# Left operands of the block products loaded into the tile of their low part, and a fourth raw tile for the right operands

## The chip, the core and the metric

The kernel runs on one core of a Trainium2 chip. Five engines work side by side on the core: TensorE (matrix products), VectorE (called DVE in the profile), ScalarE (ACT), GpSimd (POOL) and SyncE (SP), which here issues nearly all transfers between device memory and the on-chip memory. Each engine works through its own list of instructions in order, and semaphores order them against each other. The metric is the time of one execution on the device, in microseconds (us); a smaller time is better.

## The reference

One layer of a decoder trunk with three parallel groups of heads and a final normalisation, in float32, on 1024 tokens of width 2048:

```python
h = rmsnorm(x, ln_g)
proj = h @ w_in                                   # 1024 x 2048 by 2048 x 6672
g_u, g_v, g_z, d_q, d_k, d_v, d_z, d_a, d_b, c_q, c_z = split(proj)
out_a = gmlp_spatial_gating(g_u, g_v, ...) * silu(g_z)
q, k, v = causal_conv_silu([d_q, d_k, d_v])       # then l2norm of q and k
out_b = rmsnorm(gated_delta_rule(q, k, v, g, beta)) * silu(d_z)
mk, mv = split(rmsnorm(mem) @ w_mem_kv)
out_c = softmax(c_q mk^T / sqrt(128)) mv * silu(c_z)
x = x + concat(out_a, out_b, out_c) @ w_out       # 1024 x 2048 by 2048 x 2048
y = rmsnorm(x, final_g)
```

Most of the arithmetic lies in the two large products, `h @ w_in` and the one with `w_out`. The delta rule is a chunked scan with small triangular inverses; the rest is elementwise work.

## The kernel before

A float32 product is made of three faster products. Each operand is split into a high part, a copy rounded to the type float32r, and a low part, the operand minus its high part. High by high, high by low and low by high are added up (`triple`, line 445, three matmuls). So each operand of the large products costs a ScalarE cast for the high part and a VectorE subtraction for the low part (`split_to`, line 422).

The kernel first makes the memory's keys and values and a part of the projections the plain way, along with the delta rule's first heads. The remaining columns of `h @ w_in`, in five pairs of column blocks, and the whole product with `w_out`, in two pairs, go through `seven` (line 1306): a two-by-two block product made with seven block products in place of eight. Each of the seven has a left operand (activations, or sums of two halves of them, which lie ready in device memory) and a right operand (blocks of weights, or sums and differences of blocks, which are made on the chip). A block product has a sum over 1024, taken in four chunks of two 128-row blocks. Per chunk one left tile of 128 x 1024 and one right tile of 128 x 1024 are loaded and split, and 24 matmuls of 512 columns follow. There are 7 x 5 + 14 = 49 block products, so 196 chunks.

The tiles that a chunk goes through are rings, taken in turn:

- the left operand is loaded into a raw tile (`araw`, line 1265, three tiles), and split into a high tile (`ah4`) and a low tile (`al4`, line 1258, three of each): `loaded` (line 1339) does both
- the right operand is loaded into a raw tile (`wraw2`, line 1266, three tiles), perhaps summed there with kept blocks, and split into `whi3` and `wlo3` (lines 1267 and 1268, three of each) by `split_r` (line 1359)

The tiles reuse the memory of the earlier stage, whose activation tiles are `ahq` and `alq` and whose weight tiles are `kvraw`, `kvhi`, `kvlo` and `zgb`. `heir` (line 347) makes a tile in the place of an older one, and such a tile's first write waits for every use of the old one. `halves` gives the two halves of a tile and `over` makes a ring of a list. In the profile the raw tiles are named `raws` and, where the memory of `alq[2]` is used, `y`; the high tiles `ahi`; the low tiles `alo`, with the third in memory of `ahi`. The right ones are `wraw` and `y`, `whi` and `zh`, `wlo` and `zl`.

The order of the instructions on each engine is not the order in which the program names them. All operations are collected first, and `Plan.issue` (line 222) runs a model of the engines over them: an operation becomes ready when what it depends on is done in the model; among those ready, an engine takes the lowest rank and then the earliest. The loads have rank 4, the splits rank 2, the large matmuls rank 9. The order so found is then issued, engine by engine, which is why nearly every instruction bears line 277. SyncE's transfers stand in this order too, in one list.

Of the kernel before, what the change touches and what calls it, by code (L numbers as in the profile page):

```python
# [9 lines left out]
F32 = mybir.dt.float32  # L10
F32R = mybir.dt.float32r
# [11 lines left out]
HT = 512  # L23
# [39 lines left out]
class Plan:  # L63
# [21 lines left out]
    @contextmanager  # L85
    def rank(self, cls):
        old, self.cls = self.cls, cls
        yield
        self.cls = old
# [191 lines left out]
def kernel(  # L281
# [32 lines left out]
    def C(shape, name, dt=F32):  # L314
        return sb.tile(list(shape), dt, name=name, tag=name)[:]
# [31 lines left out]
    def heir(old, name, tag, n=4 * HT, dt=F32):  # L347

        t = sb.tile([P, n], dt, name=name, tag=tag)[:]
        R.users[t.tensor.name] = []  # L350
        R.heir[t.tensor.name] = old.tensor.name
        return t
# [14 lines left out]
    alq = [C([P, NT, 4, P], f"alo{q}", F32R) for q in range(NQ)]  # L367
# [7 lines left out]
    kvraw = [*wraw.bufs]  # L375
    kvhi, kvlo = [*whi.bufs], [*wlo.bufs]
# [8 lines left out]
    zgb = ring["zg"].bufs  # L385
# [36 lines left out]
    def split_to(hi, lo, src, eng):  # L422
        S.copy(hi, src)
        eng.tensor_tensor(out=lo, in0=src, in1=hi, op=ALU.subtract)
# [145 lines left out]
    for k in range(KT):  # L570
# [4 lines left out]
        hi, lo = kvhi[k % 2], kvlo[k % 2]  # L575
        with rank(2):
            for sl in kv_parts(k):
                raw = kvraw[k % 4][:, sl]
# [44 lines left out]
    for mt in range(2):  # L623
        t = [ring["ai"](F32R) for _ in range(2)]
# [9 lines left out]
    for h in range(NX):  # L634
        t = ring["vs"](F32R).rearrange("p (s m) -> p s m", s=2)
# [83 lines left out]
    def over(bufs):  # L719
        r = Ring("", 0, None)  # L720
        r.bufs = bufs
        return r
# [530 lines left out]
    def halves(t):  # L1253
        n = t.shape[1] // 2
        return [t[:, i * n : (i + 1) * n] for i in range(2)]

    ah4, al4, third = (halves(t.rearrange("p t k c -> p (t k c)")) for t in (ahq[0], alq[0], ahq[1]))
    ah4, al4 = over([*ah4, third[0]]), over([*al4, third[1]])
    raws = halves(heir(alq[1], "raws", "alo1"))
    ywide = [heir(o, f"y{i}", tag)  # L1260
             for i, (o, tag) in enumerate(((ahq[2], "ahi2"), (alq[3], "alo3"), (ahq[3], "ahi3"), (alq[2], "alo2")))]
    yu, yz, obs = ([t[:, k * HT : (k + 1) * HT] for k in range(4)] for t in ywide[:3])
    ob = over(obs)
    more = halves(ywide[3])
    araw = over([[t] for t in (*raws, more[0])])
    wraw2 = over([*kvraw[:2], more[1]])
    whi3 = over([*kvhi, heir(zgb[0], "zh", "zg0", 2 * HT, F32R)])
    wlo3 = over([*kvlo, heir(zgb[1], "zl", "zg1", 2 * HT, F32R)])
    kept = [[ring[tag](slot=k) for k in range(2)] for tag in ("kT", "qT", "kd", "ai")]
    vs01 = [ring["vs"](slot=k) for k in range(2)]  # L1270
    for tag in ("kT", "qT", "vs", "kd", "ai"):
# [9 lines left out]
    def load2(ts, src):  # L1281

        if len(ts) == 1:
            Q.dma_start(ts[0].rearrange("p (k n) -> p k n", n=HT), src)
        else:
            for t, x_ in zip(ts, src):
                Q.dma_start(t, x_)
        return ts

    def split2(srcs, hi, lo):  # L1290

        with rank(2):
            for i, t in enumerate(srcs):
                n = t.shape[1]
                split_to(hi[:, i * n : (i + 1) * n], lo[:, i * n : (i + 1) * n], t, V)
        return hi, lo
# [40 lines left out]
                takes[key](t, bank[t])  # L1337

    def loaded(src):
        with rank(4):  # L1340
            raw = load2(araw(), src)
        return split2(raw, ah4(), al4())

    def h_left(m, js):
        if m in SUM:
            return loaded(two(s2_d[0][js[0] // 2][SUM[m]]))
        j = js[0] + NH * (m in (2, 4))
        return loaded(two((hT_d if m == 4 else h0_d)[j : j + 2]))

    def m_left(m, js):  # L1350
        if m in SUM:
            return loaded(two(s2_d[1][js[0] // 2][SUM[m]]))
        return loaded(two(mix2_d[m == 4][(set1 if m == 1 else set2)[js[0]] // 2]))
# [248 lines left out]
    for n, (tag, to) in enumerate((("gt", mkT), ("inv", mv))):  # L1602
        for i in range(NX // 2):
            t = ring[tag](F32R).rearrange("p (h s m) -> p h s m", h=2, s=2)
# [190 lines left out]
```

## Time and profile before

| | |
|---|---|
| median of 3 runs | 1629.68 us (1628.36 to 1630.73) |
| the profiled execution | 1633.32 us, of which the span is 1631.6 us |
| TensorE busy | 1613.6 us (99%), 8570 matmuls |
| VectorE, ScalarE busy | 1319.3 us (81%), 1025.9 us (63%) |
| granted TensorE clock | 0.997 |
| moved by DMA | 419.44 MB, a mean of 257 GB/s |

The span is the time from the first to the last instruction of that one execution. The profile has the busy time of each engine, the chain of work that ended last, groups of like instructions with their mean time and what ended the idle time before them, and a timeline. A timeline's row has a start, a length, the engine, the operation and the tiles it writes and reads, and how often it stands there in a row (x2). "SPq" is SyncE's list of transfers: its rows are the issues, not the transfers themselves. A matmul's length in the rows (0.39 us) is that of its way through a pipeline; the next one starts 0.23 us after it.

### The profile page before, as it was taken

The page shows a single profiled execution, that of the slowest core. Times are in us where ns is not written, and L with a number is a line of the kernel's source. Part 1 is how long each engine was busy: PE and PEld are TensorE (multiplying, and loading weights), DVE is VectorE, ACT ScalarE, POOL GpSimd, SP SyncE. Part 2 cuts the span into 40 slices and gives each one's busy share as a digit, 9 for nine tenths or more (in the row PEclk, how much of TensorE's full clock was granted, in tenths as well). Part 3 has the DMA queues.
Part 4 walks back from the last instruction along what each step waited for, and adds up shares of the span by engine and source line. Part 5 has one row for each costly group of instructions (what it writes and reads, how often), then busy time and mean ns, then how long its engine had stood idle before and what let it go on. Part 6 is the DMA issues. An engine that isn't in the chain of part 4 may idle for free.

```text
span 1631.6 us, 25647 instructions
## 1 busy us (share of the span) xinstructions
PE 1613.6 (99%) x8570; PEld 1354.7 (83%) x8570; DVE 1319.3 (81%) x2288; ACT 1025.9 (63%) x2235; POOL 114.7 (7%) x139
## 2 busy tenths in 40 slices
PE   8999999999999999999999999999999999999997
PEld 6888888888888888888888888888888888888886
DVE  4876786858879869899999998888778897678875
ACT  5958674676755356877686547766657774344355
POOL 0100110020210000100101001001000000000001
PEclk9999999999999999999999999999999999999999
DMA  7888896886886867589867967889768889678646
GB/s 247 248 256 268 262 307 179 264 264 204 284 297 212 278 207 236 186 288 342 285 223 257 344 214 232 283 279 305 261 216 283 272 291 332 202 270 301 213 147 240
DMA packets 316846, 419.44 MB, mean 257 GB/s; under 512 B 51821, under 2 KB 140582, under 8 KB 316714
## 3 DMA queue, kind: packets, MB, share of 16 engines
q1 hardware_dynamic: 315010, 414.65, 77.8%
q0 software_dynamic: 1088, 2.10, 0.5%
q8 instruction: 67, 1.10, 0.3%
q10 hardware_dynamic: 616, 1.07, 0.2%
q14 instruction: 65, 0.53, 0.1%
HBM read 334.33 MB, written 82.87 MB: 256 GB/s over the span
## 4 chain that ended last, share of the span: by engine, by line
PE 95%; DMA 2%; DVE 2%; issue 1%; ACT 0%; POOL 0%; POOLq 0%; SPq 0%; DVEq 0%; ACTq 0%
PE acc L277 73%; PE dn L277 22%; DMA raws<-sd 1%; DMA kT<-in_mem_dram 1%; DVE wlo L277 1%; DVE alo L277 0%; DMA el<-vd 0%; DMA late<-kd 0%; DMA wraw<-in_w_in_dram 0%; DVE kT L277 0%; DVE kd L277 0%; ACT whi L277 0%; POOL small L277 0%; ACT jk L277 0%; DVE xr L277 0%
## 5 line engine op out<-in xcount | busy, mean ns | idle before, releaser
L277 PE MATMUL acc<-ahi,whi 128*128 128x512 f32 (+1 forms) x1152 | 451.4, 392 | 0.6 <-ACT whi L277 0.5
L277 PE MATMUL acc<-alo,whi 128*128 128x512 f32 (+1 forms) x1152 | 450.7, 392 | 0.0
L277 PE MATMUL acc<-ahi,wlo 128*128 128x512 f32 (+1 forms) x1152 | 450.0, 391 | 0.4 <-DVE wlo L277 0.4
L277 PEld LDWEIGHTS acc<-ahi,whi 128*128 128x128 f32 x1152 | 216.8, 188 | 42.0 <-ACT whi L277 1.0
L277 PEld LDWEIGHTS acc<-ahi,wlo 128*128 128x128 f32 x1152 | 216.8, 188 | 41.4 <-DVE wlo L277 0.6
L277 PEld LDWEIGHTS acc<-alo,whi 128*128 128x128 f32 x1152 | 216.9, 188 | 40.2
L277 PE MATMUL acc<-ahi,zh 128*128 128x512 f32 x736 | 233.6, 394 | 0.0
L277 ACT CAST whi<-wraw 128x512 fp32r<-128x512 f32 (+1 forms) x170 | 137.0, 807 | 102.3 <-PE acc L277 69.0
L277 ACT CAST ahi<-raws 128x1024 fp32r<-128x1024 f32 x131 | 137.4, 1049 | 84.0 <-PE acc L277 37.5
L277 DVE TENSOR_TENSOR alo<-raws,ahi 128x1024 fp32r<-128x1024 f32 x131 | 160.2, 1223 | 36.6 <-ACT ahi L277 36.0
L277 DVE TENSOR_TENSOR wlo<-wraw,whi 128x1024 fp32r<-128x1024 f32 (+1 forms) x138 | 134.5, 975 | 38.8 <-ACT whi L277 32.0
L277 PEld LDWEIGHTS acc<-ahi,zh 128*128 128x128 f32 x736 | 137.6, 188 | 27.1
L277 PE MATMUL acc<-ahi,zl 128*128 128x512 f32 x368 | 145.1, 394 | 0.0
L277 DVE TENSOR_TENSOR ahi<-y,ahi 128x1024 fp32r<-128x1024 f32 x65 | 79.3, 1220 | 21.3 <-ACT ahi L277 20.9
L277 ACT CAST ahi<-y 128x1024 fp32r<-128x1024 f32 x65 | 68.1, 1048 | 40.9 <-PE acc L277 23.0
L277 PEld LDWEIGHTS acc<-ahi,zl 128*128 128x128 f32 x368 | 69.3, 188 | 13.0
L277 ACT CAST zh<-wraw 128x1024 fp32r<-128x1024 f32 x36 | 37.8, 1049 | 43.8 <-PE acc L277 26.5
L277 POOL TENSOR_TENSOR hs<-hs,mhalf 128x4 f32<-128x4 f32 x32 | 48.0, 1502 | 234.3 <-DVE hs L277 223.8
L277 PE MATMUL dn<-whi,alo 128*128 128x512 f32 x152 | 59.0, 389 | 0.0
L277 PE MATMUL dn<-wlo,ahi 128*128 128x512 f32 x152 | 59.0, 389 | 0.0
L277 PE MATMUL dn<-whi,ahi 128*128 128x512 f32 x152 | 58.9, 389 | 0.0
L277 POOL TENSOR_TENSOR small<-small,mhalf 128x1 f32<-128x1 f32 x26 | 17.5, 677 | 581.5 <-DVE small L277 575.3
(408 smaller groups left out, 3210.4 us busy)
## 6 DMA issues: line engine op xcount, KB each, us to landing
wraw<-in_w_in_dram SPq DMA_DIRECT2D x86, 512.0 KB
raws<-sd SPq DMA_DIRECT2D x74, 512.0 KB
wraw<-in_w_in_dram SPq DMA_DIRECT2D x96, 256.0 KB
y<-in_w_in_dram SPq DMA_DIRECT2D x42, 512.0 KB
y<-sd SPq DMA_DIRECT2D x38, 512.0 KB
wraw<-in_w_out_dram SPq DMA_DIRECT2D x32, 512.0 KB
raws<-h0d SPq DMA_DIRECT2D x27, 512.0 KB
low<-wlo SPq DMA_DIRECT2D x32, 256.0 KB
```

The source lines that it names most:

```text
L277: o.fn(*o.args, **o.kw)
```

## The change

```diff
-    ah4, al4 = over([*ah4, third[0]]), over([*al4, third[1]])
-    raws = halves(heir(alq[1], "raws", "alo1"))
+    ah4, al4 = [*ah4, third[0]], [*al4, third[1]]
+    raws = halves(heir(alq[1], "raws", "alo1", dt=F32R))
...
-    araw = over([[t] for t in (*raws, more[0])])
-    wraw2 = over([*kvraw[:2], more[1]])
-    whi3 = over([*kvhi, heir(zgb[0], "zh", "zg0", 2 * HT, F32R)])
-    wlo3 = over([*kvlo, heir(zgb[1], "zl", "zg1", 2 * HT, F32R)])
+    wraw2 = over([*kvraw[:2], more[1], more[0]])
+    ah4, al4 = over([ah4[2], *ah4[:2]]), over([raws[0], al4[2], raws[1], *al4[:2]])
+    whi3 = over([heir(zgb[0], "zh", "zg0", 2 * HT, F32R), kvhi[1], kvhi[0]])
+    wlo3 = over([heir(zgb[1], "zl", "zg1", 2 * HT, F32R), kvlo[1], kvlo[0]])
...
     def loaded(src):
+        hi, lo = ah4(), al4()
         with rank(4):
-            raw = load2(araw(), src)
-        return split2(raw, ah4(), al4())
+            raw = load2([lo.bitcast(F32)], src)
+        return split2(raw, hi, lo)
```

There are no raw tiles for the left operands any more. A left operand is loaded into the low tile it will have; the cast reads it there, and the subtraction writes the low part over it. Two of the three raw tiles become low tiles, which makes five, and the third becomes a fourth raw tile for the right operands. The three high tiles stay. The rings start with other tiles than before: the left ones with those in memory of `ahq[1]` and `alq[1]`, the right ones with those in memory of `zgb`. The memory in use, the transfers and the instructions stay the same in number and shape.

## The prediction

> **What bounds the kernel now.** I read the page's first lines and its chain first, then the busy time by stretches, then who kept TensorE waiting, and last the timelines of the queues that the change touches.
>
> ```profile
> span 1631.6 us, 25647 instructions
> PE 1613.6 (99%) x8570; PEld 1354.7 (83%) x8570; DVE 1319.3 (81%) x2288; ACT 1025.9 (63%) x2235; POOL 114.7 (7%) x139
> PEclk9999999999999999999999999999999999999999
> PE 95%; DMA 2%; DVE 2%; issue 1%; ACT 0%; POOL 0%; POOLq 0%; SPq 0%; DVEq 0%; ACTq 0%
> ```
>
> TensorE is busy 99% of the span at the full granted clock, and 95% of the chain that ended last is its own instructions. DVE at 81% comes next. Where the missing 18 us of TensorE lie is seen in the stretches (columns: length, busy time and instructions of each engine, granted clock, DMA share, GB/s):
>
> ```profile
> 0.00:12.00 12.00, 5.53 (x20) 4.03 (x21) 4.07 (x6) 4.75 (x6) 1.35 (x9) 1.00 0.75 233
> 12.00:396.00 384.00, 382.85 (x2188) 325.09 (x2188) 275.81 (x628) 262.39 (x698) 39.92 (x44) 1.00 0.84 251
> 396.00:500.00 104.00, 103.97 (x608) 87.81 (x607) 87.85 (x161) 74.18 (x183) 16.04 (x15) 1.00 0.82 278
> 500.00:700.00 200.00, 198.88 (x1025) 166.47 (x1024) 168.57 (x264) 119.37 (x236) 9.74 (x15) 1.00 0.69 225
> 700.00:1000.00 300.00, 300.00 (x1470) 249.60 (x1470) 282.02 (x470) 196.70 (x378) 25.79 (x29) 1.00 0.82 273
> 1000.00:1350.00 350.00, 349.36 (x2062) 295.82 (x2062) 287.94 (x470) 238.82 (x549) 17.02 (x19) 1.00 0.83 275
> 1350.00:1623.00 273.00, 273.00 (x1205) 225.84 (x1203) 210.60 (x289) 127.62 (x184) 4.26 (x7) 1.00 0.70 240
> 1623.00:1632.00 9.00, 0.07 (x1) 0.00 (x0) 2.39 (x5) 2.06 (x4) 0.55 (x1) 0.67 0.74 270
> ```
>
> The changed loads begin at 396 us (row below). From there to 1623 us TensorE's idle time is 0.03 + 1.12 + 0 + 0.64 + 0 = 1.79 us; the other 16.5 us lie before 396 us (6.47 + 1.15) and in the tail (8.9), which the change does not touch. In 1350 to 1623 us 1205 matmuls start in 273.00 us, one each 227 ns, so the busy time there hides no slack.
>
> The waits of TensorE say the same by cause (total us, times, longest):
>
> ```profile
> PE dn L277 <- DMA kT<-in_mem_dram: 5.0, 2, 4.8
> PE dn L277 <- DVE ai L277: 1.1, 1, 1.1
> PE acc L277 <- DVE wlo L277: 0.6, 2, 0.4
> PE dn L277 <- DMA el<-vd: 0.6, 1, 0.6
> PE acc L277 <- ACT whi L277: 0.5, 1, 0.5
> ```
>
> No wait for a left operand is among them. A chunk of the block products is two 128-row blocks of the sum, 4 x 2 x 3 = 24 matmuls, at 227 ns 5.44 us; the changed stage issues 196 of them.
>
> **The change part by part.** The life of a left operand, from the timelines of SyncE, ScalarE and VectorE (start, length, operation, and in brackets the idle time before):
>
> ```profile
> 396.06 0.88 SPq L277 DMA_DIRECT2D raws<-h0d  x2
> ...
> 1429.80 0.37 SPq L277 DMA_DIRECT2D raws<-sd  x1
> ```
> ```profile
> 400.22 1.04 ACT L277 CAST ahi<-raws 128x1024 fp32r<-128x1024 f32 x1
> ...
> 1427.04 1.06 ACT L277 CAST ahi<-raws 128x1024 fp32r<-128x1024 f32 x1 [3.44 <-PE acc L277]
> 1432.48 1.05 ACT L277 CAST ahi<-raws 128x1024 fp32r<-128x1024 f32 x1 [3.43 <-PE acc L277]
> ...
> 1443.41 1.05 ACT L277 CAST ahi<-raws 128x1024 fp32r<-128x1024 f32 x1 [3.49 <-issue]
> ```
> ```profile
> 1428.56 1.22 DVE L277 TENSOR_TENSOR alo<-raws,ahi 128x1024 fp32r<-128x1024 f32 x1
> ```
>
> *When a left load starts.* Now it waits for its raw tile, that is for the split three chunks earlier: the subtraction of 1428.56 ends at 1429.78, the load goes at 1429.80. The cast of that operand comes at 1443.41, 13.6 us later. The casts at 1432.48 and 1443.41 are two chunks apart (10.93 us) and the first is released by TensorE: what a cast waits for is its high tile, free when the products three chunks earlier are done. After the change the load waits for its low tile, free when the products five chunks earlier are done. Those end two chunks before the cast's release, at about 1432.5 us: the load starts 2.7 us later and has 10.9 us instead of 13.6 us until its cast. The first load of the stage went from issue to cast in 4.16 us (396.06 to 400.22), so 6.8 us remain; and behind the cast lie two more chunks until the first matmul. So the later start costs nothing while that cover holds. Without any of it the price is 2.7 us once, since later loads follow in step.
>
> *The splits.* 131 + 65 casts and as many subtractions stay, in the same shapes. The subtraction now writes over the operand it reads. The trace has that form once, in the refill of the operand tiles, beside the same shape from another tile:
>
> ```profile
> L277 DVE TENSOR_TENSOR alo<-raws,ahi 128x1024 fp32r<-128x1024 f32 x131 | 160.2, 1223 | 36.6 <-ACT ahi L277 36.0
> L277 DVE TENSOR_TENSOR ahi<-y,ahi 128x1024 fp32r<-128x1024 f32 x65 | 79.3, 1220 | 21.3 <-ACT ahi L277 20.9
> L277 DVE TENSOR_TENSOR alo<-alo,ahi 128x512 fp32r<-128x512 f32 x16 | 10.8, 676 | 1.3 <-ACT ahi L277 1.2
> L277 DVE TENSOR_TENSOR alo<-tn,ahi 128x512 fp32r<-128x512 f32 x16 | 10.3, 683 | 0.3 <-ACT ahi L277 0.3
> ```
>
> 676 against 683 ns: I take no difference. At the worst 2 x 7 ns x 196 = 2.7 us of VectorE either way, spread over 1227 us under a full TensorE: 0 on the path.
>
> *The fourth raw tile for the right operands.* A right load may start one chunk, 5.44 us, earlier. What it can win is bounded by TensorE's idle time from 396 us on, 1.79 us, were all of it due to late rights; it is bounded below by a loss of the same kind, an early load in front of one that is needed first (priced in the slower rival). I take 0, nearest to the 0.6 + 0.5 us that TensorE waited for right tiles.
>
> *The other order of the first tiles.* It moves which tile the first few splits at 400 us take. TensorE's idle time from 396 to 500 us is 0.03 us: nothing to win, and a loss of at most one load's flight, 4.16 us, if the first pair came late. The first left tile and its load are the same as before, so I take 0.
>
> *SyncE's queue.* It issues all these loads in one written order, and a load that waits holds whatever stands behind it (total us, times, longest):
>
> ```profile
> SPq L277 <- DVE wlo L277: 177.5, 101, 7.1
> SPq L277 <- DVE alo L277: 167.5, 92, 5.5
> SPq L277 <- DVE ahi L277: 88.5, 42, 5.0
> SPq L277 <- PE acc L277: 36.5, 32, 4.5
> ```
>
> The two rows for the left splits (167.5 + 88.5 us) turn into waits for TensorE. 196 issues stay 196, with the same bytes. The written order is made anew by the planner, from its own model, so also TensorE's order of small and large products may shift a little; a changeover costs about 0.1 us (timeline of TensorE: the start after it comes 0.33 us later instead of 0.23):
>
> ```profile
> 992.34 0.69 PE L277 MATMUL dn<-tblk,gt 32*32 32x32 f32 x32
> 992.97 0.50 PE L277 MATMUL acc<-alo,whi 128*128 128x512 f32 x1
> 993.30 0.40 PE L277 MATMUL acc<-ahi,wlo 128*128 128x512 f32 x1
> ```
>
> The sum against the profiled execution: 1633.32 + 0 + 0 + 0 + 0 = 1633.32 us (span 1631.6). It stands 3.64 us above the median of the runs, 1629.68; on the median the forecast is no change, which I write as 1629.5.
>
> [...]
>
> **The rivals.** *Slower: the queue holds up a transfer without slack.* Not all transfers have the left operand's cover. In the chain two places show a left load going straight ahead of a transfer that TensorE ends up waiting for, or of the work before it:
>
> ```profile
> 999.56 5.26 DMA raws<-sd
> ...
> 1004.84 6.19 DMA el<-vd
> ...
> 1011.07 1.16 PE dn L277 x8
> ...
> 1235.50 4.67 DMA raws<-sd
> ...
> 1243.66 1.18 PE dn L277 x8
> ```
>
> If the left load in the queue waits 2.7 us longer, what stands behind it is that much later, and here the matmul after it as well. The two places here, and the 1.1 us wait for ai as a third, give 3 x 2.7 = 8.1 us: 1637.8. It decides from about the second such place on, since 2 x 2.7 = 5.4 us is over 0.2% (3.3 us, about what a measurement of this kernel can tell from no change). Against it: the planner knows of the new wait when it orders the queue. Chance 0.28. [...]
>
> *Faster: earlier rights and a luckier order.* All of 1.79 us, plus changeovers saved. Over 0.2% takes 1.5 us more, fifteen changeovers of 0.1 us. With twenty it is 1629.68 - 1.79 - 2.0 = 1625.9. For it: DVE is busy 282.02 of 300 us from 700 to 1000, where earlier rights would let it work ahead; against it: TensorE idles 0.00 us in that very stretch. Chance 0.14.
>
> *The change does nothing at all*, since rights were never late: then the time is 1629.68 too, and it is part of the likeliest case (0.58).
>
> **How the numbers follow.** No change, 1629.5, with its own range of 3.3 us to each side: 1626.4 to 1633. Slower 0.28 and faster 0.14 are the rivals' chances. The range reaches below to 1625, leaving out a little more than a third of the faster case (0.06), and above to 1638, just over the slower rival's price, leaving out half of that case (0.14).
>
> **What would show it.** Right: TensorE's idle time from 396 to 1623 us under 4 us, its busy time within 3 us of 1613.6, the casts of the left tiles still released by TensorE, the left loads released by TensorE instead of VectorE and about 11 us ahead of their casts. Wrong on the slower side: rows in which TensorE waits for el, ai or left tiles, some us each. Wrong on the faster side: busy time well under 1611 with the same instructions. The prediction fails if the new written order differs by far more than the moved waits do.

## The result and the profile after

The changed kernel takes 1635.19 us (median of 13 runs, 1631.36 to 1637.62) against 1630.40 us for the kernel before on the same chip (13 runs, 1628.36 to 1632.40): a ratio of 1.0027 [1.0021, 1.0034], 4.8 us slower. The forecast was 1629.5 us and no change, with 0.28 on slower; the range, 1625 to 1638, holds the time.

The profiled execution of the changed kernel took 1635.8 us, that of the kernel before 1633.32 us. The first lines and the chain of the changed kernel's page:

```profile
span 1634.1 us, 25742 instructions
PE 1615.0 (99%) x8570; PEld 1355.3 (83%) x8570; DVE 1318.9 (81%) x2288; ACT 1021.7 (63%) x2235; POOL 107.8 (7%) x139
PEclk9999999999999999999999999999999999999999
PE 95%; DVE 2%; DMA 1%; ACT 1%; issue 1%; POOL 0%; POOLq 0%; SPq 0%; ACTq 0%; DVEq 0%
```

Nothing there speaks: the same 99%, the same 8570 matmuls. The stretches of the changed kernel (columns as in the prediction: length, busy time and instructions of TensorE, its weight loads, VectorE, ScalarE and GpSimd, granted clock, DMA share, GB/s) say little more:

```profile
12.00:396.00 384.00, 381.95 (x2184) 323.71 (x2184) 276.53 (x630) 263.32 (x700) 41.26 (x45) 1.00 0.84 252
396.00:500.00 104.00, 103.74 (x595) 86.45 (x595) 84.70 (x154) 67.08 (x167) 12.54 (x13) 1.00 0.82 268
...
1000.00:1350.00 350.00, 348.18 (x2100) 296.16 (x2100) 284.66 (x458) 239.34 (x550) 13.51 (x18) 1.00 0.81 270
1350.00:1623.00 273.00, 273.00 (x1206) 226.15 (x1205) 211.18 (x289) 126.08 (x182) 3.72 (x6) 1.00 0.70 240
```

The idle time from 396 to 1623 us is 2.14 us (0.26 + 0.00 + 0.06 + 1.82 + 0.00) after 1.79 before. A lesson stands here already: idle time undercounts what a wait costs. A matmul's row is 0.39 us long while the next one starts 0.23 us after it, so the first 0.16 us of a wait still look busy, and matmuls at half the clock look busy all the time (3.41 of 3.41 us in the stretch at half clock below). So I also worked out from the starts of TensorE's matmuls how much each stretch lost against the usual spacing of the same kinds of matmul, and compared the profiled executions (us more than the kernel before; e9, e13 and e18 are experiments below; the first 350 us, in which nothing was changed, are left out):

| stretch | changed | e9 | e13 | e18 |
|---|---|---|---|---|
| 350 to 400 | +1.2 | +1.2 | +0.1 | -0.1 |
| 400 to 650 | +1.2 | +0.6 | -0.1 | +1.1 |
| 650 to 700 | -1.4 | -1.5 | +0.2 | 0.0 |
| 700 to 1000 | 0.0 | +0.6 | +0.4 | +0.7 |
| 1000 to 1050 | +3.0 | +1.9 | +1.5 | -1.0 |
| 1050 to 1350 | -0.9 | -0.9 | +3.6 | +1.9 |
| sum | +3.2 | +1.9 | +5.6 | +2.7 |

The changed kernel loses most at two places, near 392 us and near 1012 us, and wins back the 1.1 us wait for ai, which is gone. The 1.2 us between 400 and 650 us come in pieces of under 0.4 us each and are not explained here. The waits of TensorE by cause (total us, times, longest) name the two:

```profile
PE dn L277 <- DMA el<-vd: 1.8, 1, 1.8
...
PE acc L277 <- ACT xr L277: 0.9, 1, 0.9
```

*At 392 us.* The new first right tile, zh, can be written earlier than the old one, so the planner puts its cast into ScalarE's list ahead of the copy that frees TensorE's accumulator. TensorE's and ScalarE's timelines of the changed kernel:

```profile
392.33 0.39 PE L277 MATMUL acc<-ahi,wlo 128*128 128x512 f32 x1
393.65 0.50 PE L277 MATMUL acc<-ahi,whi 128*128 128x512 f32 x1 [0.93 <-ACT xr L277]
```
```profile
389.00 1.04 ACT L277 CAST zh<-wraw 128x1024 fp32r<-128x1024 f32 x1
...
393.03 1.05 ACT L277 COPY xr<-acc 128x512 f32<-128x512 f32 x2
```

From start to start 1.32 us in place of 0.23: 1.1 us lost. ScalarE has work without a break from the cast to the copy, so its 1.04 us push the copy back.

*At 1012 us.* TensorE waits for a small transfer, and the matmuls behind it are 0.43 us apart in place of 0.23:

```profile
1011.97 1.16 PE L277 MATMUL dn<-wsT,el 128*128 128x128 f32 x8 [1.82 <-DMA el<-vd]
...
1015.08 0.63 PE L277 MATMUL acc<-ahi,zh 128*128 128x512 f32 x1
1015.51 0.63 PE L277 MATMUL acc<-alo,zh 128*128 128x512 f32 x1
```

The granted clock in two stretches of 3.41 us shows why (same columns as above; the clock is the third number from the end):

```profile
1010.04:1013.46 3.42, 1.60 (x14) 1.49 (x14) 2.19 (x4) 1.12 (x3) 0.00 (x0) 1.00 0.84 262
1013.46:1016.87 3.41, 3.41 (x12) 2.83 (x12) 1.15 (x2) 1.43 (x3) 0.00 (x0) 0.50 0.91 304
```

After a wait of 1.82 us TensorE ran 3.41 us at half the clock, which costs 1.7 us. The kernel before waits 0.56 us at the same matmul and keeps its clock (1.00 from 1010 to 1017 us). So 1.3 + 1.7 = 3.0 us, the whole loss of that stretch. Why el came later, in SyncE's queue (changed kernel, then kernel before):

```profile
1003.50 0.43 SPq L277 DMA_DIRECT2D ahi<-sd  x1
1004.03 0.41 SPq L277 DMA_DIRECT2D raws<-sd  x1
1004.54 0.41 SPq L277 DMA_DIRECT2D wraw<-in_w_in_dram  x1
1005.04 0.42 SPq L277 DMA_DIRECT2D xd<-y  x1
1005.51 0.43 SPq L277 DMA_DIRECT2D el<-vd  x1
```
```profile
1003.27 0.42 SPq L277 DMA_DIRECT2D raws<-sd  x1
1003.79 0.42 SPq L277 DMA_DIRECT2D xd<-y  x1
1004.84 0.33 SPq L277 DMA_DIRECT2D el<-vd  x1
```

Two left loads and a right one stand shortly ahead of it in place of one left load, and it goes 0.67 us later; TensorE, for its part, is ready 0.36 us earlier (1010.15 against 1010.51 us).

### The profile page after: what moved, and what is told of

Read it like the earlier page. It is cut to its first block, busy times and chain, and to the rows that moved or that the text cites. A ratio compares the mean times of both kernels' runs of the same rounds, so it can differ in the third digit from the quotient of the medians.

```text
span 1634.1 us, 25742 instructions
## 1 busy us (share of the span) xinstructions
PE 1615.0 (99%) x8570; PEld 1355.3 (83%) x8570; DVE 1318.9 (81%) x2288; ACT 1021.7 (63%) x2235; POOL 107.8 (7%) x139
## 4 chain that ended last, share of the span: by engine, by line
PE 95%; DVE 2%; DMA 1%; ACT 1%; issue 1%; POOL 0%; POOLq 0%; SPq 0%; ACTq 0%; DVEq 0%
PE acc L277 73%; PE dn L277 21%; DVE wlo L277 1%; DMA wraw<-in_w_mem_kv_dram 0%; DMA el<-vd 0%; DVE kT L277 0%; ACT whi L277 0%; DVE alo L277 0%; DVE y L277 0%; DMA kT<-in_mem_dram 0%; ACT jk L277 0%; DVE kd L277 0%; DVE inv L277 0%; ACT tn L277 0%; POOL small L277 0%
## 5 line engine op out<-in xcount | busy, mean ns | idle before, releaser
L277 PE MATMUL acc<-alo,whi 128*128 128x512 f32 (+1 forms) x696 | 271.8, 391 | 0.0
L277 PE MATMUL acc<-ahi,zh 128*128 128x512 f32 x448 | 164.9, 394 | 0.0
L277 PEld LDWEIGHTS acc<-alo,whi 128*128 128x128 f32 x696 | 131.0, 188 | 23.6
L277 DVE TENSOR_TENSOR wlo<-wraw,whi 128x512 fp32r<-128x512 f32 (+1 forms) x118 | 110.1, 934 | 47.8 <-ACT whi L277 39.9
L277 DVE TENSOR_TENSOR alo<-alo,ahi 128x1024 fp32r<-128x1024 f32 (+1 forms) x94 | 106.0, 1128 | 31.0 <-ACT ahi L277 30.4
L277 ACT CAST ahi<-alo 128x1024 fp32r<-128x1024 f32 (+1 forms) x94 | 91.4, 974 | 54.2 <-PE dn L277 21.0
L277 PE MATMUL acc<-raws,whi 128*128 128x512 f32 x296 | 116.5, 394 | 0.0
L277 DVE TENSOR_TENSOR raws<-raws,ahi 128x1024 fp32r<-128x1024 f32 x79 | 96.4, 1220 | 10.2 <-ACT ahi L277 9.8
L277 ACT CAST whi<-y 128x1024 fp32r<-128x1024 f32 x55 | 57.8, 1050 | 37.0 <-PE acc L277 20.2
L277 DVE TENSOR_TENSOR wlo<-y,whi 128x1024 fp32r<-128x1024 f32 x55 | 67.1, 1220 | 13.8 <-ACT whi L277 13.7
L277 PE MATMUL acc<-whi,ahi 128*128 128x512 f32 x176 | 65.3, 390 | 0.0
```

The costliest lines, as they stand in the source:

```text
L277: o.fn(*o.args, **o.kw)
```

## The experiments

Three theories. **A**: the loss is the new written order, at the two places above. **B**: the tiles themselves, since left loads that wait for TensorE hold up SyncE's queue (the slower rival of the prediction). **C**: any newly planned order is a draw, and the order before was a lucky one.

### The parts, and the late transfer (e1 to e4)

e1 is the changed kernel once more. e2 and e3 separate the order of the right tiles from the rest; e2:

```diff
-    whi3 = over([heir(zgb[0], "zh", "zg0", 2 * HT, F32R), kvhi[1], kvhi[0]])
-    wlo3 = over([heir(zgb[1], "zl", "zg1", 2 * HT, F32R), kvlo[1], kvlo[0]])
+    whi3 = over([*kvhi, heir(zgb[0], "zh", "zg0", 2 * HT, F32R)])
+    wlo3 = over([*kvlo, heir(zgb[1], "zl", "zg1", 2 * HT, F32R)])
```

e3 is the kernel before with the reverse of this edit. e4 tells the planner's model that the loads of vd take longer, so that it puts the products on them later:

```diff
-        Q.dma_start(vg, v_d[hf][g])
+        Q.dma_start(vg, v_d[hf][g]).lat = 4000.0
```

> The changed kernel once more, for a second profile and its ratio on this chip. Theory A (two places): the cost sits in two waits of TensorE, one at about 392 us (for the copy xr, 1.1 us) and one at about 1012 us (for el, 1.8 us, and then 3.4 us at half clock). Both should be there again, and the ratio again about 1.003. Theory B (the queue): left loads that now wait for the products hold up SyncE's queue in many places, and TensorE's lost time is spread over the stage. Theory C (a new order by chance): the waits lie elsewhere in this second look, and the ratio is within 1.001.

> The changed kernel with the old order of the right operands' high and low tiles (zh and zl last instead of first). Theory A: the early cast of zh no longer stands ahead of the copy xr, the wait at 392 us is gone, and the time falls by 1.1 us or somewhat more, ratio about 1.002; the wait for el may stay. Theory B: nothing changes, 1.003. Theory C: anything within 0.3% either way, with waits in new places.

> The kernel before with only the new order of the right operands' high and low tiles (zh and zl first). Left operands as before, three raw tiles each. Theory A: the wait of about 1.1 us for xr at 392 us appears and the ratio is about 1.0007. Theory B: no such wait, ratio 1.000. Theory C: anything within 0.3%.

> The changed kernel, with the planner told that the load of el takes 4 us longer to land than it assumed, so that the products on it are put later in TensorE's list. Theory A: the wait for el and the half clock after it are gone, 3.0 us less (1.3 us of wait more than before the change, 1.7 us of half clock), ratio about 1.001. Theory B: the hold-ups move to the next transfer without slack and the ratio stays near 1.003. Theory C: within 0.3% either way.

| run | median, us | before on the same chip | ratio |
|---|---|---|---|
| e1 | 1636.22 | 1630.27 | 1.0034 [1.0021, 1.0046] |
| e2 | 1635.71 | 1630.27 | 1.0030 [1.0019, 1.0040] |
| e3 | 1631.05 | 1630.27 | 1.0006 [0.9997, 1.0015] |
| e4 | 1637.83 | 1630.27 | 1.0049 [1.0036, 1.0061] |

e1 repeats both waits (0.9 us for xr, 2.9 us for el, with half the clock behind it: the eight small matmuls on el run 1.79 us there and 1.16 in e11). e3 has the wait at 392 us with none of the rest of the change, and so shows that the order of the right tiles is enough for it:

```profile
391.58 0.50 PE L277 MATMUL acc<-ahi,whi 128*128 128x512 f32 x1 [1.13 <-ACT xr L277]
```

It costs that kernel nothing that can be measured. In e2 that wait is gone, but the el wait is 2.8 us, and TensorE waits 2.5 us in all for whi: the loss is the same without the new right order. In e4 the el wait is gone too, and a new one stands elsewhere, in e4's own new order, again with half the clock (at 1402 us; the matmuls from 1402.70 on start 0.43 us apart):

```profile
1402.11 0.79 PE L277 MATMUL acc<-whi,ahi 128*128 128x512 f32 x1 [2.50 <-ACT ahi L277]
```

So each edit that lets the planner order everything anew takes away one wait and brings another. That points to C, and asks how much an order alone can do.

### Orders drawn anew (e5 to e8, e16, e17)

Both kernels with one constant of the planner's model changed by a trifle; nothing else differs. e5 and e7 (kernel before, changed kernel), then e6 and e8, then e16 and e17:

```diff
-    SEEN = {"pe": 55.0, "act": 35.0, "dve": 35.0, "pool": 78.0, "sp": 60.0}
+    SEEN = {"pe": 55.0, "act": 35.0, "dve": 35.0, "pool": 78.0, "sp": 90.0}
```
```diff
-    DMA_FIXED = 1600.0
+    DMA_FIXED = 1650.0
```
```diff
-    SEEN = {"pe": 55.0, "act": 35.0, "dve": 35.0, "pool": 78.0, "sp": 60.0}
+    SEEN = {"pe": 55.0, "act": 35.0, "dve": 35.0, "pool": 78.0, "sp": 75.0}
```

> The kernel before, with one of the planner's constants moved by a hair (the delay after which SyncE sees a semaphore, 60 to 90 ns in the model), so that all lists from about the first stage on are ordered anew with the same tiles. Theory C (the order by chance): the order before was a good draw, and this one is slower by 0.1% to 0.4%, with waits of TensorE in new places and perhaps a stretch at half clock. Theory B (the left loads in SyncE's list): the tiles are the cause, so this stays within 0.1% of before, ratio 0.999 to 1.001.

> The kernel before with another constant of the planner's model moved (a transfer's fixed time, 1600 to 1650 ns). The same as for the first new order of it: theory C 1.001 to 1.004, theory B 0.999 to 1.001.

> The changed kernel with the same small move of the planner's constant (60 to 90 ns). Theory C: the time is a new draw, anywhere from 0.999 to 1.005, and it overlaps with the two new orders of the kernel before. Theory B: 1.002 to 1.004 again, with TensorE waiting for el or another small transfer behind left loads in SyncE's list.

> The changed kernel with the other move (1600 to 1650 ns). Theory C: anywhere from 0.999 to 1.005. Theory B: 1.002 to 1.004 again, the same waits.

> The kernel before, planned anew: one constant of the planner's model is other by 15 ns (SyncE sees a release after 75 ns instead of 60). Order by chance: somewhere from 1.000 to 1.009, as the two re-plans before it (1.0038, 1.0095). If the order before is robust: 0.999 to 1.001.

> The changed kernel, planned anew with the same constant. If the tiles cost nothing on average: between 1.000 and 1.009, as likely below as above the re-plan of the kernel before. If they cost: above it by 0.002 or more.

| planner's model | tiles of before | changed tiles |
|---|---|---|
| as it is | 1 | 1.0027 [1.0021, 1.0034], again 1.0034 |
| SyncE sees 90 ns | 1.0038 [1.0026, 1.0050] (e5) | 1.0081 [1.0068, 1.0094] (e7) |
| transfers fixed 1650 ns | 1.0095 [1.0081, 1.0110] (e6) | 1.0052 [1.0039, 1.0064] (e8) |
| SyncE sees 75 ns | 1.0067 [1.0050, 1.0084] (e16) | 1.0132 [1.0112, 1.0152] (e17) |

With the old tiles three trifles cost 0.4 to 1.0%, each more than the change. Behind the start, the longest wait is for E in e6 and e17 (4.7 and 4.3 us), of which neither the kernel before nor the changed kernel has a row. And e5, with the old tiles, has both waits of the changed kernel, for the copy xr at 392 us and for el at 1010 us; the waits of e5:

```profile
PE dn L277 <- DMA el<-vd: 1.7, 1, 1.7
...
PE acc L277 <- ACT xr L277: 1.3, 1, 1.3
```

So both places can turn into waits by the written order alone, without the changed tiles. The mean granted clock of that execution of e5 was 0.999, against 0.996 in the profiled one of the changed kernel.

So the order before was a good draw: none of the seven other orders in this table reaches it, nor do those of e2 and e4; only e3 comes near. Whether the changed tiles cost something on top these pairs don't settle: +0.30 (the mean of the two), +0.43, -0.43 and +0.65%, a mean of +0.24% with a standard error of 0.23% (the standard deviation of the four, 0.47, divided by two).

### The two places mended, the order otherwise kept (e9 to e12)

Here no new order is drawn. Named operations are put later in the written order, with what depends on them:

```diff
-        self.ops.sort(key=lambda o: (o.at, o.idx))
+        put_later(self.ops, {**{i: 1011300 for i in range(9323, 9327)}, **{i: 1015350 for i in range(9336, 9340)}}); self.ops.sort(key=lambda o: (o.at, o.idx))
...
+def put_later(ops, by):
+    def later(o, t):
+        for b in (o, *o.tail):
+            if b.at < t:
+                b.at = t
+                for n in b.succ:
+                    later(n, t)
+
+    for i, t in by.items():
+        later(ops[i], t)
```

That is e9: 9323 to 9326 are the four products on el, 9336 to 9339 the four on tn. e10 adds `4389: 391450`, the cast into zh. e11 is the kernel before with `{9322: 1001500}`, the load of el; e12 is the kernel before with the six products on inv at 688 us (5491 to 5496), the products on el and those on tn put later.

> The changed kernel with the written order kept as it is, except that the four products on el at about 1012 us stand 15 small and large matmuls later in TensorE's list (behind the four transposes of tn), and the four on tn 14 large matmuls later. If the loss of the changed kernel is what this one place of its order costs (order by chance), the wait for el (1.8 and 2.9 us in the two profiles) and the half clock behind it (3.4 us long, 1.7 us of cost) go: 3.5 to 4.5 us less than the changed kernel, ratio to the kernel before 1.0003 to 1.0010, and no half clock between 900 and 1100 us. If the arrangement of the tiles itself costs the time (left loads that hold up SyncE's queue), the time moves elsewhere and the ratio stays at 1.0027 to 1.0034.

> As the run before, and the cast of the first right tile into zh at 389 us moved behind the two copies of xr in ScalarE's list. Order by chance: the wait for xr (0.9 us; 1.1 us lost from start to start) goes too, and with both places mended the changed tiles are as fast as the kernel before: ratio 0.9995 to 1.0005. If the arrangement of the tiles costs: over 1.002.

> The kernel before with its order kept, except that the load of el stands behind two more small transfers in SyncE's list (some 1.4 us later); no other engine's list differs. If the changed kernel lost its time in that thin place, the same loss appears here without any of the changed tiles: the wait for el grows from 0.56 us to 1.5 to 2.5 us, half clock of 3.4 us follows it, together 2.5 to 3.7 us more, ratio 1.0015 to 1.0023. If a wait of that size does not bring the half clock: 1.0008 to 1.0012. If the place has slack after all: 1.000.

> The kernel before with its order kept, except that its own two waits are given cover: the six products on inv at 688 us (wait of 1.12 us for ai) seven large matmuls later, and the four products on el at 1011 us (wait of 0.56 us) three large matmuls later. Order by chance: what TensorE waits in the middle can be mended place by place: 1.0 to 1.7 us less, ratio 0.9990 to 0.9994, which would be under both kernels; no half clock. If TensorE then waits a step later for the same thing: 1.000.

| run | median, us | before on the same chip | ratio |
|---|---|---|---|
| e9 | 1633.41 | 1630.48 | 1.0016 [1.0006, 1.0026] |
| e10 | 1633.49 | 1630.48 | 1.0016 [1.0006, 1.0026] |
| e11 | 1631.73 | 1630.48 | 1.0006 [0.9994, 1.0019] |
| e12 | 1630.18 | 1630.48 | 0.9996 [0.9987, 1.0006] |

e9 does what was wanted at its place: no wait for el, no half clock (large matmuls in a row start 0.23 us apart from 1012 to 1020 us). It gives back less than expected (1.0016 where 1.0003 to 1.0010 stood), since at 1025 us a wait appears that was not there; the waits of e9:

```profile
PE dn L277 <- DVE states L277: 1.5, 1, 1.5
...
PE acc L277 <- ACT xr L277: 0.9, 1, 0.9
```

In the table above the stretch from 1000 to 1050 us falls from +3.0 to +1.9. e10 halves the wait for xr (0.5 us) and wins nothing beyond e9. So mending the place at 1012 us gives back 1.8 us of the medians' 4.8, a little under half, though the intervals of the two ratios overlap (1.0021 to 1.0026). Where the rest lies was not shown, since new waits came with the edits. e11 missed too: it lengthened the wait for el to 1.3 us only, and without half the clock (the matmuls behind it start 0.23 us apart). e12 has the smallest time of all, 0.3 us under the kernel before, inside its interval: 0.9 us of wait for ai remain, where it was 1.1. No version beats the kernel before by a measurable amount.

### The tiles and the order taken apart (e13, e14, e15, e18)

Both kernels consist of the same 13591 operations, one for one, so each can be issued in the other's order. Only where the tiles forbid it must an operation go later:

```diff
-        self.ops.sort(key=lambda o: (o.at, o.idx))
+        take_order(self.ops, TIMES); self.ops.sort(key=lambda o: (o.at, o.idx))
...
+    for o in ops:
+        o.at = at[o.idx] / 10
...
+    for o in sorted(ops, key=lambda o: (o.at, o.idx)):
+        for n in o.succ:
+            if n.at < o.at:
+                later(n, o.at + 400.0)
```

TIMES is the list of planned times from the other kernel, `later` is as above. e13 is the changed kernel with the times of before. Of its operations 177 are put later, 172 left loads and 5 right ones, by 2.8 us on average (120 of them change places with other transfers in SyncE's list); the lists of TensorE, ScalarE, VectorE and GpSimd are those of the kernel before. e14 is the reverse. e15 is e13 with 2900.0 in place of 400.0. That does less than its expectation says: in the plan the 177 loads stand only 1.0 us further back on average, 15 of them the full 2.5 us, because a load put 2.9 us behind the first use that it must follow is often behind the later ones already. e18 is e13 with the left loads taken out of SyncE's queue:

```diff
-            raw = load2([lo.bitcast(F32)], src)
+            raw = [lo.bitcast(F32)]
+            G.dma_start(raw[0].rearrange("p (k n) -> p k n", n=HT), src)
```

> The changed tiles, but every operation is issued at the place that it has in the kernel before; only what the new tiles forbid is moved later. TensorE's, ScalarE's, VectorE's and GpSimd's lists are then those of the kernel before, instruction for instruction; of SyncE's 1376 transfers 120 stand later. If the order makes the loss: ratio 0.9990 to 1.0007, the waits of before (ai about 1 us, el 0.5 to 1.5 us), no wait for xr, no half clock in the middle. If the tiles make it (left loads that wait for TensorE hold up what stands behind them): 1.002 to 1.004, with TensorE waiting for transfers that were in time before.

> The tiles of the kernel before, every operation at the place that it has in the changed kernel; only what the old tiles forbid is moved later: 166 of SyncE's 1376 transfers, 39 of VectorE's 2288 operations and 1 of ScalarE's 1947, and TensorE's list is that of the changed kernel. If the order makes the loss: ratio 1.0020 to 1.0045, with waits for el of 1.5 us or more at about 1012 us and half clock behind it. If the tiles make it: 0.9990 to 1.0010.

> The changed tiles in the order of the kernel before, as in the run before this one, but each of the 177 left loads that the new tiles forbid at its old place stands 2.5 us further back in SyncE's list, so that it asks for its tile when TensorE is mostly done with it. No other engine's list changes. If the loss of that run (1.0037) came from loads that waited at the head of SyncE's queue and held the small transfers behind them: SyncE's waits for TensorE fall well under 399.6 us, the waits of TensorE for steps (2.3 us) and tn (1.9 us) go, and the ratio is 0.9990 to 1.0010. If the later load itself is the cost, since its cover is gone: TensorE waits for left tiles, ratio over 1.004.

> The changed tiles in the order of the kernel before, as in e13, but the 196 left loads are issued by GpSimd, so that a left load that waits for TensorE holds nothing of SyncE's list. If the hold of the queue made the loss of e13 (1.0037): SyncE's waits for TensorE fall under 100 us, the waits of TensorE for tn (1.9 us) and steps (2.3 us) go, ratio 0.9985 to 1.0015. If the later start of the left loads made it: still 1.003 to 1.005. A third outcome would be a price of GpSimd's own queue: its small operations (7% of the span) wait behind the loads, and TensorE waits for what they write (xr, hs, E): over 1.005.

| run | median, us | before on the same chip | ratio |
|---|---|---|---|
| e13 | 1638.22 | 1631.11 | 1.0037 [1.0024, 1.0050] |
| e14 | 1921.48 | 1631.11 | 1.1781 [1.1758, 1.1805] |
| e15 | 1638.11 | 1631.53 | 1.0040 [1.0025, 1.0056] |
| e18 | 1633.15 | 1631.05 | 1.0015 [1.0006, 1.0024] |

e13 went against the theory that I then held, C alone. With every other engine's list that of the kernel before, the later loads cost 7.1 us of the median (6.0 us by the ratio). The waits of TensorE in e13, and of SyncE's queue:

```profile
PE dn L277 <- DVE steps L277: 2.3, 1, 2.3
PE dn L277 <- DMA tn<-vd: 1.9, 1, 1.9
```
```profile
SPq L277 <- PE acc L277: 399.6, 153, 7.0
```

How a left load makes TensorE wait for steps is seen in the queue, first of the kernel before, then of e13:

```profile
1184.11 0.33 SPq L277 DMA_DIRECT2D mixd<-vs  x1
1184.49 0.42 SPq L277 DMA_DIRECT2D vs<-gd  x1
...
1190.40 0.40 SPq L277 DMA_DIRECT2D vs<-mixd  x1
```
```profile
1187.18 0.33 SPq L277 DMA_DIRECT2D mixd<-vs  x1
1187.61 0.39 SPq L277 DMA_DIRECT2D raws<-sd  x1
1188.04 1.94 SPq L277 DMA_DIRECT2D vs<-gd  x1
...
1195.63 0.38 SPq L277 DMA_DIRECT2D alo<-sd  x1
1196.06 0.46 SPq L277 DMA_DIRECT2D vs<-mixd  x1
```

The first store comes 3.07 us later, as late as TensorE is there anyway (3.08 us). Then a left load stands in between, the issue behind it takes 1.94 us in place of 0.42, and from the first store to the load of vs from mixd it is 8.88 us in place of 6.29. VectorE, which makes steps from vs, waits for that load, and TensorE for steps: 2.3 us.

In e18 the same left loads start as late as in e13 (12.2 us ahead of their cast, against 12.0, in the median of the 196), but hold nothing of SyncE's list. The waits of e18 for these causes, and its SyncE queue's:

```profile
PE dn L277 <- DVE steps L277: 0.8, 1, 0.8
```
```profile
SPq L277 <- PE dn L277: 57.0, 33, 6.2
...
SPq L277 <- PE acc L277: 41.2, 31, 9.2
```

The wait for tn is gone, that for steps 0.8 us, and the loss is 2.1 us in place of 7.1 (by the ratios 2.4 in place of 6.0). So 3.6 to 5 us of e13's loss were the hold of the queue: B is a real mechanism, with about that price in that order. The two ratios were measured beside the same kernel before but not in the same set of runs, and their intervals just meet at 1.0024. What the remaining 2 us are is not settled: the start 2.8 us later, or GpSimd's queue, which took these loads up.

e15 missed. With the loads 1.0 us further back, SyncE waits less (324.6 us for the accumulators in place of 399.6), and steps is no longer among the waits over half a microsecond; but the wait for tn stays (1.6 us), and others come in its place; the waits of e15:

```profile
PE acc L277 <- ACT y L277: 1.7, 4, 0.9
PE dn L277 <- ACT vs L277: 1.6, 2, 1.4
PE dn L277 <- DMA tn<-vd: 1.6, 1, 1.6
```

So this smaller move exchanged some waits for others; loads that all stand 2.5 us further back were not tried. e14 tells nothing about the theories: the old tiles forbid the new order so often (206 operations out of their places, the worst 31 us later) that the result is an order that nobody would plan.

For the changed kernel itself, then: most of what its profile shows as lost lies at the two places of its own new order (shown by the trace; a little under half of the loss removed by e9), and an order over the old tiles can have waits at the same two places (e5). At one of them two left loads stand ahead of the late transfer, in the manner of B, but that they caused it was not shown: e11 moved that transfer in the kernel before and got a wait of 1.3 us, without a loss that can be measured. How much of the 0.27% another draw of the order would spare stays open, since draws differ by 0.4 to 1.0% themselves.

## Why the prediction was wrong, step by step

- *When a left load starts* (2.7 us later, with 10.9 us until its cast). Right: in e13 the loads that must move do so by 2.8 us in the plan, and in the last stretch of the changed kernel a load goes 10.66 us ahead of its cast, which TensorE releases as before:

```profile
1429.73 0.37 SPq L277 DMA_DIRECT2D alo<-sd  x1
```
```profile
1440.39 1.05 ACT L277 CAST ahi<-alo 128x1024 fp32r<-128x1024 f32 x1 [3.44 <-PE acc L277]
```

- *So the later start costs nothing while that cover holds.* True of the left tiles: TensorE waits for none of them. Wrong of the kernel, because the cover was counted for the load alone and not for what stands behind it in the same queue. The waits of SyncE's queue in the changed kernel show the move from VectorE to TensorE that the prediction described:

```profile
SPq L277 <- PE acc L277: 274.7, 154, 7.0
SPq L277 <- DVE wlo L277: 165.4, 96, 5.1
SPq L277 <- PE dn L277: 84.1, 56, 5.0
```

- *SyncE's queue, set at 0.* This is the first step that failed, and e13 and e18 show it for the old order; for the changed kernel's own order it stays open. The slower rival had the mechanism and nearly the price: three places at 2.7 us, 8.1 us, stood against 6.0 to 7.1 us in e13, where only loads moved. That the sums are so near is luck in part. Of its places one was right in kind (the small transfers around 1012 us); the largest, steps at 1204 us, it had not named. It was given 0.28, against it "the planner knows of the new wait", and the range holds the measured time only because it was drawn up to this rival's price. The planner's new order did not save the time: 1.0027 and 1.0034 against 1.0037 in the old order.
- *The written order may shift a little, about 0.1 us per changeover.* The second step that failed, and the one that the trace of the changed kernel itself shows. The new order has its own waits of 0.9 and 1.8 us and a half clock: 3.0 us at 1012 us, where the sum had 0. e5 has both waits with the old tiles, and orders with unchanged tiles differ by 0.4 to 1.0%. What the prediction named last, a new order that differs by more than the moved waits, should have been a rival with a price; the plan's thinness could be seen before, in transfers such as el, which landed 0.56 us too late already.
- *The other order of the first tiles, set at 0, bound 4.16 us.* Mis-sized: it costs 1.1 us at 392 us, in the changed kernel as in e3, from a cast on ScalarE and not from a late load. The row that I took, idle time from 396 us on, begins behind the place: the ring's first tile is cast at 389 us.
- *The splits in place.* Right: 1220 ns for the subtraction over its own operand, in the rows of the changed kernel, against 1223 ns before.

```profile
L277 DVE TENSOR_TENSOR raws<-raws,ahi 128x1024 fp32r<-128x1024 f32 x79 | 96.4, 1220 | 10.2 <-ACT ahi L277 9.8
```

- *The fourth raw tile, at 0.* No run separates it. TensorE's waits for right tiles are 0.6 us for wlo and 0.5 for whi, as before.
- *The clock.* Neither the sum nor the price of a rival had a term for it. In the changed kernel a wait of 1.82 us was followed by 3.41 us at half the clock, which cost 1.7 us.
- *What would show it.* "Idle time under 4 us, busy time within 3 us" came true (2.14 us; 1615.0 against 1613.6) while the kernel got slower. Of the signs on the slower side, a wait for el did come, 1.8 us. The signs for "right" were too coarse: 1.4 us more of busy time look like more work, and matmuls at half the clock count as busy.

## What to carry to other kernels

A transfer that waits later in an in-order queue is priced by the transfers behind it (e13 lost 6.0 us by the ratio, e18 with the same loads out of the queue 2.4), so its own slack is not the bound; list what stands behind it and how late that may be. Where a planner writes the order anew, the order is a term of its own: draw it a few times with a trifle changed before a difference of a few tenths of a per cent is put down to an edit, or keep the order and move single operations. Do not take busy time as proof that nothing was lost (at half the clock TensorE was busy for all of 3.41 us and lost 1.7 of them): compare the starts of the matmuls and the granted clock around each wait.

## What the runs showed of the hardware

Where the half clock stood: at 18.44 and 1626.12 us in the profile of the kernel before, at 16.76, 1013.46 and 1627.86 us in that of the changed kernel. The three stretches that ended before the kernel did were 3.41 us long, and the distances within a profile, 1607.68, 996.70 and 614.40 us, are 471, 292 and 180 times 3.4133 us. Divide both profiles into pieces of that length, counted from these starts. Between 50 and 1600 us seven pieces hold more than 0.3 us of idle time of TensorE: 0.94, 0.34, 0.77 and 0.56 us in the kernel before, 0.93, 0.93 and 1.82 us in the changed kernel. The piece with 1.82 us was followed by half the clock, the other six were not (clock 1.00). In e7 a stretch of 3.41 us with 2.74 us idle was followed by it too:

```profile
393.10:396.51 3.41, 0.67 (x3) 0.21 (x2) 1.68 (x5) 2.77 (x9) 1.91 (x2) 1.00 0.85 304
396.51:399.92 3.41, 3.22 (x8) 2.55 (x9) 3.41 (x8) 2.55 (x8) 0.00 (x0) 0.50 0.01 4
```

The length of a wait alone does not tell its price: after the 1.82 us in the changed kernel the clock was 0.50, while in e13 it stayed at 1.00 after the 2.34 us for steps, which lay in two stretches (idle 0.87 and 1.47 us). That the place of the wait decides is my estimate from these cases; the stretches of e13:

```profile
1198.83:1202.25 3.42, 2.55 (x13) 1.95 (x11) 0.14 (x1) 0.47 (x1) 0.00 (x0) 1.00 0.80 280
1202.25:1205.66 3.41, 1.94 (x9) 1.48 (x10) 3.03 (x5) 2.77 (x8) 0.00 (x0) 1.00 0.56 175
1205.66:1209.08 3.42, 3.42 (x22) 2.94 (x22) 2.95 (x7) 1.10 (x5) 0.00 (x0) 1.00 0.66 247
```

The first half-clock stretch began at 16.76 us in one profile and at 18.44 us in the other, so the same wait can lie otherwise in another execution. By my estimate that is one source of the spread between runs of one kernel: of the 35 runs of the kernel before beside e9 to e12, those with a mean granted clock of 0.999 took 1629.3 us on average (14 runs), of 0.998 1630.8 (15), of 0.997 1632.4 (5), and the one of 0.996 1636.2. A stretch of 3.41 us at half the clock lowers that mean by 0.001 (1.7 of 1631 us) and, as above, costs 1.7 us.
